# Float32 products with values, moved into one row behind their transpositions and copies

## The chip, the cores and the metric

The kernel runs on one core of one Trainium2 chip. The metric is the device time of one execution in microseconds, and the figure compared is the median over several executions. Five engines work side by side, each through its own queue and in the order of that queue: TensorE (PE in the profile; its weight loads are shown apart as PEld), VectorE (DVE), ScalarE (ACT), GpSimd (POOL) and SyncE (SP), which issues most of the transfers.

## The reference

A bidirectional encoder of two layers over 1024 tokens of width 1024, all in float32. What matters here is the mixing half of a layer: three groups of channels are computed side by side, normed, concatenated and projected.

```python
for l in range(DEPTH):
    h = _rmsnorm(x, g_pre_mix[l])
    zf, zq, zk, zv, zm = jnp.split(h @ w_in[l], splits, axis=-1)
    y_f = _fourier_mix(zf, w_fourier[l])
    q, k = _rope(zq), _rope(zk)              # 8 query heads, 2 key heads of 64
    y_a = _window_attn(q, k, v, sink[l])     # softmax(q k^T) v, window of 128 to each side, with a sink
    km, vm = split(_rmsnorm(mem, g_mem[l]) @ w_mem_kv[l])
    y_m = _memory_attn(zm, km, vm)           # softmax(q km^T) vm, 4 heads, 256 memory rows
    y = concat[_rmsnorm(y_f), _rmsnorm(y_a), _rmsnorm(y_m)] @ w_out[l]
    x = x + _rmsnorm(y, g_post_mix[l])
    gate, up = jnp.split(_rmsnorm(x) @ w_ffn_in[l], 2, axis=-1)
    x = x + _rmsnorm((silu(gate) * up) @ w_ffn_out[l])
```

## The kernel before

Tokens are cut into eight tiles of 128. Nearly every product is done as three products of float32 numbers split into a high and a low part (`split`, lines 174 to 177; class `Acc`, line 187). The products with values that this change touches are not: they multiply plain float32 operands, and the trace shows each of them as two records on PE, with 128 rows of operand and 64 columns of weight.

**Window attention.** The eight query heads form two groups of four, one for each key head. `att_units(g)` gives nine units per group; unit i forms the values of tile i-1 (`att_values`) and then the scores of tile i (`att_scores`). A tile sees nk blocks of keys, three, or two at the ends, so 22 blocks a layer. For each block j, PE transposes the four heads' probabilities into a PSUM tile `pT` (line 825, two buffers). In the first head group (g = 0) they are split and multiplied at line 840. In the second (g = 1), ScalarE copies them into one of four buffers `pf` (line 830), and for s = 0 and 1 a float32 product (line 833) adds the block's values into `av`: s = 0 writes partitions 0 to 63, s = 1 partitions 64 to 127, each 256 columns. ScalarE then takes `av` out (line 842), and `out_prep` splits it for the projection and forms its sum of squares (`ssp`, line 988).

**Memory attention.** Heads and halves of the sequence give eight score units (`mem_scores`); `mem_turn` transposes the exponentials of one head in two blocks of memory rows, mt = 0 and 1 (`mpT`, line 922), and ScalarE copies each (line 924). `mem_values(pr, half, pfs)` takes a pair of heads: four float32 products (line 932) add into `mav`, for mt = 0 and 1 and for s = 0 and 1 (the head of the pair, written to partitions 0 to 63 or 64 to 127), 512 columns each. VectorE takes `mav` out (line 933). There are four such pairs a layer.

**What sets the order.** The stages are interleaved by hand. The memory units stand beside the queries' projection (`qp`). The second head group runs in a loop that also holds, for earlier tiles, the output projection (`out`, shown as `mo`, line 187), the norms, and the transpositions for the feed-forward part (`hb.tile`, shown as `hTp`, line 1106). Within what dependencies allow, a planner then orders each engine's queue by simulated costs, work that comes earlier in the program first; an instruction that isn't ready by its costs is overtaken by later ones that are. That is how products of one tile come to stand apart on PE with other work between them:

```python
weave(mix.mem_units(), q[1:8] + [mix.fm_load] + q[8:])
...
for i in range(NT + 4):
    if i < NT + SKEW:
        att[i]()
    if 2 <= i < NT + 2:
        hs[i - 2] = mix.out(i - 2, x1d[i - 2])
    if i >= 4:
        hb.tile(hs.pop(i - 4), i - 4)
```

The accumulators of both products (`av`, `mav`) share two PSUM buffers with other users of the tag "av" (`ssp`, `qT`).

Of the kernel before, what the change touches and what calls it, by code (L numbers as in the profile page):

```python
# [19 lines left out]
P = 128  # L20
# [49 lines left out]
def tile_encoder(ctx: ExitStack, tc: tile.TileContext, T, C, out):  # L70
# [12 lines left out]
    def nm(s):  # L83
        uid[0] += 1
        return f"{s}_{uid[0]}"
# [49 lines left out]
    class Ring:  # L135


        def __init__(self, *ks):
            self.ks, self.i = ks, 0
# [28 lines left out]
    def ps(shape, name="ps", tag="pd"):  # L168
        return psp[tag].tile([P] + list(shape), F32, tag=tag, name=nm(name))

    f32 = lambda ap: ap.bitcast(F32)
    mm = nc.tensor.matmul

    def split(hi, lo, src, lo_eng=None):

        nc.scalar.copy(hi, src)  # L176
        return (lo_eng or nc.vector).tensor_tensor(out=lo, in0=src, in1=f32(hi), op=ALU.subtract)  # L177
# [334 lines left out]
                dup_stacks([(self.km[ci][:, j, 0], self.km[ci][:, j, 1]) for j in range(2)], raw[:, ci])  # L512


    class Mix:
        def __init__(self, l, hT, mem):
            self.l, self.hT, self.mem = l, hT, mem
# [299 lines left out]
        def att_values(self, g, n, es_, dst):  # L817

            k0, k1 = max(0, n - 1), min(NT, n + 2)
            nk = k1 - k0  # L820
            av = ps([512], "av", "av")
            for j in range(nk):
                pT = ps([4, P], "pT", "pT")
                for h in range(4):
                    nc.tensor.transpose(pT[:, h, :], es_[h // 2][:, h % 2, j * P : j * P + P], ident)  # L825
                if g:

                    pf = self.pfs[self.pfi % 4]
                    self.pfi += 1
                    nc.scalar.copy(pf, pT.rearrange("p (k s) q -> p s k q", s=2))  # L830
                    for s in range(2):
                        rhs = pf[:, s].rearrange("p k q -> p (k q)")
                        mm(av[64 * s : 64 * s + 64, 0 : 2 * P], self.v32[:, k0 + j], rhs, start=j == 0, stop=j == nk - 1)  # L833
                    continue
                pp = phs(2, 512, dt=F32R)
                ph, pl = pp[:, 0], pp[:, 1]
                split(ph, pl, pT.rearrange("p h q -> p (h q)"))
                lhs = self.vst[(k0 + j) // 4][:, (k0 + j) % 4, g].rearrange("p a d -> p (a d)")
                for i, p_ in enumerate((ph, pl)):
                    mm(av, lhs, p_, start=j == 0 and i == 0, stop=j == nk - 1 and i == 1)  # L840
            if g:
                nc.scalar.copy(dst, av[:, 0 : 2 * P].rearrange("p (k q) -> p k q", k=2))
            else:
                self.fold(av, dst)
# [82 lines left out]

        def mem_values(self, pr, half, pfs):
            av = ps([512], "mav", "av")
            for mt in range(2):  # L930
                for s in range(2):
                    mm(av[64 * s : 64 * s + 64], self.mem.v[:, mt, 2 * pr + s], pfs[s][mt], start=mt == 0, stop=mt == 1)  # L932
            nc.vector.tensor_copy(self.ym[half][:, pr, :], av)

        def mem_units(self):
# [483 lines left out]
    for l in range(DEPTH):  # L1419
# [4 lines left out]
        q = mix.skewed(mix.q, mix.q_turn, NT)  # L1424
# [142 lines left out]
```

## Time and profile before

| | |
|---|---|
| runs (median; lowest to highest) | 2031.55 us; 2031.51 to 2036.65 us |
| profiled execution: time, span | 2032.38 us, 2030.4 us |
| granted TensorE clock, mean over the span | 0.994 |
| VectorE, ScalarE, GpSimd busy | 74%, 52%, 34% of the span |
| memory attention with the queries' projection | about 145 to 210 us (layer 0), 1140 to 1210 us (layer 1) |
| second head group with the output projection | about 286 to 380 us (layer 0), 1285 to 1380 us (layer 1) |

The time of an execution is the span from the first to the last instruction and about 2 us around it. Busy time on PE counts the whole passage of a product through the array, so products that follow each other closely overlap in it; how long a row of them really holds PE is read from the chain of waits, or from the start of the first to the start of the next work.

### The profile page before, as it was taken

What the parts mean: (1) busy time and instruction counts of PE and PEld (TensorE: products, weight loads), DVE (VectorE), ACT (ScalarE), POOL (GpSimd) and SP (SyncE); (2) the same over time, 40 slices, a digit from 0 to 9 for tenths busy, and PEclk for the clock granted to TensorE, in tenths of its full rate; (3) what the DMA queues carried; (4) which work ended last, traced back from release to release, by engine and by line L of the source; (5) the groups of instructions that cost most, each with busy time, mean ns of one, the idle gap of its engine ahead of it and who ended that gap; (6) DMA issues with size and microseconds to landing.
All of it is one profiled execution on the core that took longest, in us unless ns stands there. A gap on an engine that the chain in (4) does not pass through costs nothing.

```text
span 2030.4 us, 28325 instructions
## 1 busy us (share of the span) xinstructions
PE 1984.7 (98%) x9587; PEld 1631.2 (80%) x9587; DVE 1492.6 (74%) x2346; ACT 1049.7 (52%) x2204; POOL 684.9 (34%) x811
## 2 busy tenths in 40 slices
PE   8999999999999999999999999999999999999998
PEld 7877878778888888887888778877788888887886
DVE  5566767897877776778876668679786776778766
ACT  6476877643333333554555768686333333346441
POOL 4344445224334333002423644451433433410011
PEclk9999999999999999999999999999999999999999
DMA  6110333434333324879831113244333323269973
GB/s 213 62 58 22 109 104 115 146 109 130 104 109 100 103 88 139 297 266 324 286 142 54 54 58 115 85 144 135 106 118 114 116 82 114 96 209 354 314 265 125
DMA packets 181889, 288.56 MB, mean 142 GB/s; under 512 B 15560, under 2 KB 81648, under 8 KB 181744
## 3 DMA queue, kind: packets, MB, share of 16 engines
q1 hardware_dynamic: 173680, 267.88, 39.7%
q10 hardware_dynamic: 8064, 18.88, 2.4%
q8 instruction: 75, 1.23, 0.2%
q14 instruction: 70, 0.57, 0.1%
HBM read 220.11 MB, written 66.58 MB: 141 GB/s over the span
## 4 chain that ended last, share of the span: by engine, by line
PE 86%; DVE 5%; DMA 3%; ACT 2%; issue 2%; POOL 1%; SPq 0%; DVEq 0%; POOLq 0%; ACTq 0%
PE fo L1330 17%; PE qc L1181 11%; PE qx L1181 11%; PE qy L1181 11%; PE mo L187 8%; PE qz L1181 5%; PE kvp L187 4%; PE qp L187 3%; PE zT L187 2%; PE sc L788 2%; PE pT L825 2%; PE av L833 1%; PE qa L1181 1%; PE mav L932 1%; PE av L840 1%
## 5 line engine op out<-in xcount | busy, mean ns | idle before, releaser
L1330 PE MATMUL fo<-arena_r 128*128 128x512 f32 x1512 | 354.2, 391 | 6.0 <-ACT big L1355 3.8
L1330 PEld LDWEIGHTS fo<-arena_r 128*128 128x128 f32 x1512 | 283.6, 188 | 65.6 <-ACT big L1355 4.6
L176 ACT CAST arena_r<-arena_f 128x512 fp32r<-128x512 f32 (+2 forms) x344 | 185.9, 571 | 179.5 <-DMA arena_f<-actd 66.6
L1181 PE MATMUL qc<-arena_r,flex 128*128 128x512 f32 x912 | 220.2, 390 | 0.0
L177 DVE TENSOR_TENSOR arena_r<-arena_f,arena_r 128x512 fp32r<-128x512 f32 x262 | 182.0, 727 | 46.9 <-ACT arena_r L176 39.0
L1171 ACT CAST flex<-arena_f 128x512 fp32r<-128x512 f32 x148 | 91.9, 621 | 235.0 <-PE qy L1181 73.3
L1181 PEld LDWEIGHTS qc<-arena_r,flex 128*128 128x128 f32 x912 | 171.2, 188 | 37.0
L1181 PE MATMUL qy<-arena_r,flex 128*128 128x512 f32 x576 | 139.9, 390 | 2.3 <-ACT flex L1171 2.3
L1171 ACT CAST arena_r<-arena_f 128x512 fp32r<-128x512 f32 x92 | 57.1, 621 | 159.1 <-DVE arena_f L1168 63.6
L1172 DVE TENSOR_TENSOR flex<-arena_f,flex 128x512 fp32r<-128x512 f32 x148 | 110.9, 750 | 28.4 <-ACT flex L1171 28.2
L1181 PEld LDWEIGHTS qy<-arena_r,flex 128*128 128x128 f32 x576 | 107.9, 188 | 25.3 <-ACT flex L1171 2.7
L1215 POOL TENSOR_TENSOR arena_f<-arena_f 128x512 f32<-128x512 f32 x36 | 47.3, 1315 | 237.5 <-ACT arena_f L1186 237.5
L1181 PE MATMUL qx<-arena_r 128*128 128x512 f32 x360 | 119.5, 389 | 0.0
L1181 PE MATMUL qy<-arena_r 128*128 128x512 f32 x480 | 116.7, 390 | 0.0
L1172 DVE TENSOR_TENSOR arena_r<-arena_f,arena_r 128x512 fp32r<-128x512 f32 x92 | 68.2, 742 | 63.2 <-ACT arena_r L1171 62.8
L1181 PE MATMUL qz<-arena_r,flex 128*128 128x512 f32 x320 | 106.8, 395 | 0.0
L1181 PEld LDWEIGHTS qy<-arena_r 128*128 128x128 f32 x480 | 90.3, 188 | 18.9 <-ACT arena_r L1171 0.2
L1168 DVE TENSOR_TENSOR arena_f<-arena_f 128x512 f32<-128x512 f32 x90 | 98.1, 1098 | 5.5 <-DMA arena_f<-in_w_ffn_in 3.9
L1222 POOL TENSOR_TENSOR arena_f<-arena_f 128x512 f32<-128x512 f32 x36 | 60.0, 1667 | 120.2 <-DVE arena_f L1221 120.2
L187 PE MATMUL mo<-big,arena_r 128*128 128x512 f32 x384 | 100.2, 399 | 0.3 <-ACT arena_f L1031 0.2
L1181 PE MATMUL qx<-flex,flex 128*128 128x512 f32 x304 | 100.1, 390 | 0.0
L1242 POOL TENSOR_TENSOR arena_f<-arena_f,flex 128x512 f32<-128x512 f32 x32 | 51.8, 1619 | 139.5 <-ACT flex L1233 83.7
(315 smaller groups left out, 4659.8 us busy)
## 6 DMA issues: line engine op xcount, KB each, us to landing
arena_f<-in_w_ffn_out SPq DMA_DIRECT2D x264, 256.0 KB, 4.7
actd<-arena_f SPq DMA_DIRECT2D x154, 256.0 KB, 2.5
arena_f<-actd SPq DMA_DIRECT2D x154, 256.0 KB, 4.4
arena_f<-in_w_ffn_in SPq DMA_DIRECT2D x46, 512.0 KB, 3.7
big<-in_w_ffn_in SPq DMA_DIRECT2D x40, 512.0 KB, 4.5
arena_f<-in_w_in SPq DMA_DIRECT2D x40, 256.0 KB, 2.9
arena_f<-in_x SPq DMA_DIRECT2D x16, 512.0 KB, 4.3
arena_f<-in_w_out SPq DMA_DIRECT2D x32, 256.0 KB, 2.7
```

The costliest lines, as they stand in the source:

```text
L176: nc.scalar.copy(hi, src)
L177: return (lo_eng or nc.vector).tensor_tensor(out=lo, in0=src, in1=f32(hi), op=ALU.subtract)
L187: mm(self.dst, a, b, start=self.i == 0, stop=self.i == self.n - 1)
L788: mm(pt, lhs, self.kst[g][i][:, k0 * P : k1 * P], start=i == 0, stop=i == 1)
L1168: nc.vector.tensor_tensor(out=s, in0=x, in1=y, op=op)
L1171: self.cast = nc.scalar.copy(w[:, 0], s)
L1172: nc.vector.tensor_tensor(out=w[:, 1], in0=s, in1=f32(w[:, 0]), op=ALU.subtract)
L1181: mm(pt, a, b, start=start and n == 0, stop=n == 11, skip_group_check=not start)
L1215: G(out=self.u2, in0=self.u2, in1=self.p1, op=ALU.add)
L1222: G(out=self.p5, in0=self.p1, in1=self.p5, op=ALU.add)
L1242: (G if i % 2 else V).tensor_tensor(out=a[i], in0=c, in1=g[i], op=ALU.mult)
L1330: mm(pt, ab[:, 0, x, sl], ab[:, 1, y], start=new and first and j == 0, stop=last and j == 2, skip_group_check=not new)
```

## The change

In the second head group, `att_values` first transposes and copies all blocks of the tile, keeping the copies in a list, and then issues the tile's products (four or six) one after the other, last block first. In `mem_values` the four products of a pair are issued in the order mt = 1, 0 and, within it, s = 1, 0. The first product issued is the one whose copy is made last. A new helper, `together`, sets the flags that open and close the accumulation: the first two products open the two halves of the partitions, the last two close them. The number and kind of instructions stay as they were.

```diff
+    def together(products):
+
+        for i, p_ in enumerate(products):
+            p_(i < 2, i >= len(products) - 2)
...
             av = ps([512], "av", "av")
+            pfs = []
             for j in range(nk):
                 pT = ps([4, P], "pT", "pT")
...
                     pf = self.pfs[self.pfi % 4]
                     self.pfi += 1
                     nc.scalar.copy(pf, pT.rearrange("p (k s) q -> p s k q", s=2))
-                    for s in range(2):
-                        rhs = pf[:, s].rearrange("p k q -> p (k q)")
-                        mm(av[64 * s : 64 * s + 64, 0 : 2 * P], self.v32[:, k0 + j], rhs, start=j == 0, stop=j == nk - 1)
+                    pfs.append(pf)
                     continue
...
             if g:
+                together([
+                    lambda start, stop, j=j, s=s: mm(
+                        av[64 * s : 64 * s + 64, 0 : 2 * P], self.v32[:, k0 + j], pfs[j][:, s].rearrange("p k q -> p (k q)"),
+                        start=start, stop=stop,
+                    )
+                    for j in reversed(range(nk)) for s in range(2)
+                ])
                 nc.scalar.copy(dst, av[:, 0 : 2 * P].rearrange("p (k q) -> p k q", k=2))
...
             av = ps([512], "mav", "av")
-            for mt in range(2):
-                for s in range(2):
-                    mm(av[64 * s : 64 * s + 64], self.mem.v[:, mt, 2 * pr + s], pfs[s][mt], start=mt == 0, stop=mt == 1)
+            together([
+                lambda start, stop, mt=mt, s=s: mm(av[64 * s : 64 * s + 64], self.mem.v[:, mt, 2 * pr + s], pfs[s][mt], start=start, stop=stop)
+                for mt in (1, 0) for s in (1, 0)
+            ])
             nc.vector.tensor_copy(self.ym[half][:, pr, :], av)
```

## The prediction

> **What bounds the kernel now.** I read the page first: the span, the engines, the chain.
>
> ```profile
> span 2030.4 us, 28325 instructions
> PE 1984.7 (98%) x9587; PEld 1631.2 (80%) x9587; DVE 1492.6 (74%) x2346; ACT 1049.7 (52%) x2204; POOL 684.9 (34%) x811
> PE 86%; DVE 5%; DMA 3%; ACT 2%; issue 2%; POOL 1%; SPq 0%; DVEq 0%; POOLq 0%; ACTq 0%
> ```
>
> TensorE is busy nearly all the time and carries 86% of the chain that ends last. Next, two stretches that hold the moved products, in the view of busy time by stretch:
>
> ```profile
> 160.00:180.00 20.00, 20.00 (x106) 14.38 (x106) 10.25 (x17) 10.04 (x32) 9.25 (x20) 1.00 0.00 1
> 290.00:372.00 82.00, 81.71 (x490) 64.03 (x488) 53.91 (x118) 60.57 (x154) 42.64 (x72) 1.00 0.33 115
> ```
>
> Behind the stretch stand its length and the busy time of PE, PEld, DVE, ACT and POOL. PE hardly rests, while the others have 20 to 50% to spare. So time that PE no longer spends here should reach the end, and time that another engine waits here costs nothing. Third, the moved products themselves: the attention's in the view of its tile, the memory part's in the view by stretch, one row a layer:
>
> ```profile
> L833 PE MATMUL av<-flex,arena_f x176: 379/379/431, 293.8 to 1369.1; 128*64 128x256 f32 x176
> ```
> ```profile
> 155.00:215.00 60.00, 11.17 (x32) 2.39 (x32) 1.00 0.11 36
> 1150.00:1215.00 65.00, 12.23 (x32) 2.57 (x32) 1.00 0.14 45
> ```
>
> A product has two records, so these are 88 products of 256 columns in attention and 16 of 512 columns in each layer's memory part, which now keep PE busy 11.17 and 12.23 us.
>
> **Two prices, from the chain of waits in order of time.** First the memory part of layer 0 (start, length, what; x2 of `mav` is one product):
>
> ```profile
> 168.29 1.01 PE mav L932 x4
> 169.30 0.59 PE mpT L922 x4
> 169.89 1.00 PE mav L932 x2
> ...
> 183.72 1.86 PE mav L932 x6
> ...
> 186.94 0.44 PE mpT L922 x4
> ...
> 198.57 1.87 PE mav L932 x8
> ...
> 205.13 1.00 PE mav L932 x2
> ```
>
> One product alone takes 1.00 us, two take 1.01, three 1.86, four 1.87. So the two that write different halves of the partitions run side by side, and PE is held by slots: 0.86 us (1.87 less 1.01) for a pair, and as much for a lone product. The rest of a piece, 1.00 - 0.86 = 0.14 us, is paid once for each stay in this shape of product.
>
> The second price is what a stay costs the work behind it. The four transposition records right behind a stay (169.30) take 0.59 us, four in peace (186.94) take 0.44: 0.15 us more. In attention:
>
> ```profile
> 286.11 2.76 PE mo L187 x12
> ...
> 293.89 0.58 PE av L833 x4
> ...
> 308.14 1.45 PE av L833 x12
> ...
> 1307.63 0.58 PE av L833 x4
> 1308.21 0.91 PE mo L187 x3
> ...
> 1368.93 0.58 PE av L833 x4
> ```
>
> Here x4 is one pair, x12 three: a pair takes (1.45 - 0.58) / 2 = 0.435 us, so a stay costs 0.145 us beside its pairs, as above. The three `mo` products behind it take 0.91 us, where twelve in peace take 2.76 (0.23 each): 0.22 us more. A stay therefore costs 0.145 + 0.15 = 0.30 to 0.145 + 0.22 = 0.37 us beside its slots. I take 0.33, as both kinds of work stand behind the groups. Weight loads and semaphores lie inside these pieces and aren't priced apart.
>
> **The change part by part.** It adds and removes no instruction, transfer or load; ScalarE's copies (lines 830, 924) and the copies out (842, 933) stay, and the queues of SP and POOL have no part in the moved products. What changes is how many stays there are and how well the slots are filled.
>
> (a) *Attention, second head group.* The chain shows 33 pieces of line 833 (16 in layer 0, 17 in layer 1; first and last quoted), all made of whole pairs. So no slot is gained. There are 16 tiles, each needs one stay: 33 - 16 = 17 stays go, 17 x 0.33 = 5.6 us. Bounds: 5.1 at 0.30, 6.3 at 0.37; nothing, if other work still cuts every tile's row.
>
> (b) *Memory, slots.* A row of four takes two slots. The pieces of layer 0, put to the four pairs of heads, hold 1+2+1, 1+3, 4 and 1+3 products, which is 3+3+2+3 slots; those of layer 1 hold 1+3 three times and 1+2+1, which is four times 3. The busy time above bears this out: 11 slots and 8 stays against 12 and 9 differ by one of each, 0.86 and about 0.2, and the rows by 12.23 - 11.17 = 1.06 us. So 23 slots against 16. Two of the seven I don't count: the lone first products of the last pairs, at 205.13 and 1204.01, fill a seam before attention in which other engines set the pace, as the timeline shows (in brackets the idle time before it, and what ended it):
>
> ```profile
> 208.70 0.58 PE L988 MATMUL ssp<-const,arena_f 128*128 128x2 f32 x4 [0.80 <-DVE arena_r L438]
> ```
> ```profile
> 1204.01 1.07 PE L932 MATMUL mav<-arena_f 128*64 128x512 f32 x2
> ```
>
> Moved from there, their 1.00 us becomes idle time. Five slots: 5 x 0.86 = 4.3 us.
>
> (c) *Memory, stays.* 8 and 9 become 4 and 4. Without the two of the seams seven go: 7 x 0.33 = 2.3 us.
>
> (d) *Waiting at the head of a row.* The first product of a row now waits for the last copy, and behind it on PE's queue wait its row and what the planner puts next (`mo`, `hTp`, `ssp`, scores). Before, each group waited for its own copy. What ended PE's idle time before line 833, weight loads included (total us, times), and the copy:
>
> ```profile
>   ACT arena_f L316: 0.5, 2
>   ACT arena_f L801: 0.5, 2
>   ACT arena_r L176: 0.3, 1
>   ACT arena_f L362: 0.2, 1
> ```
> ```profile
> L830 ACT COPY flex<-pT x44: 563/587/607, 290.4 to 1364.1; 128x512 f32<-128x512 f32 x44
> ```
>
> That is 1.5 us by ScalarE over 33 groups, 0.045 each; 24 rows at that rate are 1.1 us, no more than now. The cover is other PE work such as the 2.76 us at 286.11. Without it a row waits for one copy, 0.59 us. I take no change, nearest to the 0.045.
>
> (e) *Behind a row.* In attention the copy out (842) starts up to two pairs, 0.87 us, later after ScalarE's last copy than before. Who needs it is `out_prep`, and its result feeds an `mo` two tiles on; eight tiles fill the 82 us stretch, so that is some 20 us away. The `pf` buffers are read later too, but a buffer comes up again only with the next tile's second copy, some 10 us on. Both cost nothing while a tile takes that long; without that cover it would be 0.87 us a tile.
>
> (f) *Rows that don't hold.* Work earlier in the program that becomes ready can still get in between. Of 24 rows I expect two or three to be cut: 0.8 us back.
>
> Sum: 5.6 + 4.3 + 2.3 - 0.8 = 11.4 us. The profiled execution took 2032.38 us (its span and 2 us around it), 0.83 above the median of the runs. 2032.4 - 11.4 = 2021.0 for it; from the median 2031.55 it is 2020.1. I say 2020.
>
> **A rule weighed: the clock.** The kernel shows stretches of 3.4 us at half clock behind ones in which PE rested about half the time (the third last column is the granted clock):
>
> ```profile
> 370.50:374.00 3.50, 1.67 (x15) 1.16 (x12) 3.06 (x6) 2.24 (x6) 2.99 (x4) 1.00 0.62 199
> 374.00:377.40 3.40, 3.40 (x14) 3.02 (x13) 3.40 (x6) 2.14 (x4) 0.52 (x2) 0.50 0.70 189
> 205.80:209.20 3.40, 2.60 (x18) 1.93 (x17) 3.33 (x8) 2.77 (x5) 1.34 (x3) 1.00 0.46 150
> ```
>
> At half speed a stretch costs half of 3.40, 1.7 us. In the seam at 207 PE is busy 2.60 of 3.40 us; with the lone product gone from there the idle time comes near 0.80 + 1.00 = 1.8 us, and the first row has 3.50 - 1.67 = 1.83. So one more half-clock stretch is possible, and elsewhere one less: the sum would be 9.7 or 13.1. The Trainium skill ("TensorE: Matmul & The Clock Gate", Part 1) puts the half rate behind an idle window of about 3.4 us; by that a gap of 1.8 us costs nothing and the sum stays 11.4. The rows above contradict it: the clock fell after 1.83 us of rest.
>
> **The rivals.**
>
> *The rows are cut (faster or no change).* The planner orders PE's queue, so products may stay apart. If all attention rows are cut as now, (a) and its share of (f), 0.5, go: 11.4 - 5.1 = 6.3 us, 2025.3. For it: the 33 pieces for 16 tiles. Against: 308.14 x12 and 198.57 x8 are whole rows, where all copies were there; the new order makes that the rule.
>
> *The gain is given back (no change).* PE gets ahead and others become late: ScalarE with 60.57 us in 82, DVE and POOL with 10.25 and 9.25 in 20. For it: the seams, where the chain leaves PE already. Against: 0.29 us of idle PE in 82 us. If half is lost: 2031.55 - 5.7 = 2025.9.
>
> *Rows wait for their copies (slower).* PE's queue is in order. ScalarE's too: a last copy can stand behind exponentials (line 801 ended some of the waits above) or behind the copy before it. At one copy of 0.59 us for each of 24 rows, 14.2 us are lost against 12.2 won (before (f)): 2033.6. At two, 28.3: 2047.6. It decides from 0.51 us a row, and 0.76 make it slower by 0.3%. Against it: 0.045 us a group now, and that the last copy had to be waited for before as well.
>
> **How the numbers follow.** A measurement of this kernel tells about 0.3%, 6.1 us, from no change; faster means below 2025.4. The sum as worked out 0.66; rows cut 0.11, half of it on the faster side; given back 0.11; rows that wait 0.12, of which 0.10 beyond 0.3%. Faster 0.72, same 0.18, slower 0.10. Low end: all seven slots and nine stays of the memory part at 0.37 (6.0 + 3.3), (a) at 6.3 and one half-clock stretch less, 1.7: 17.3, so 2014. High end: the second rival with another half-clock stretch and half of (a) cut, 2030; what lies above is mostly the third.
>
> **What would show it.** Right: line 833 in 16 pieces of 1.01 or 1.45 us, line 932 in eight of 1.87, as many PE instructions as before; the feed-forward part of layer 0 starts about 5 us earlier, that of layer 1 about 11. Wrong: over 20 pieces of line 833; ScalarE ending more than 5 us of PE's idle time before it; more stretches at 0.50; DVE and ACT rising in the chain between 150 and 380 us. It fails above all if the new order moves what the planner places behind it, which nothing in the trace before can show.

## The result and the profile after

The changed kernel takes 2018.07 us (median of 6 runs, 2013.64 to 2025.46), the kernel before 2032.17 (6 runs): a ratio of 0.993, 95% interval 0.9914 to 0.9946. On a second chip session it was 0.9939 (0.9916 to 0.9962). Predicted were 2020 us and a range of 2014 to 2030. The page of the profiled execution, the fastest of the six with 2013.64 us:

```profile
span 2011.7 us, 28335 instructions
PE 1968.4 (98%) x9587; PEld 1627.5 (81%) x9587; DVE 1492.5 (74%) x2346; ACT 1049.0 (52%) x2204; POOL 686.2 (34%) x811
PE 83%; DVE 6%; DMA 3%; issue 3%; ACT 2%; POOL 2%; SPq 0%; DVEq 0%; POOLq 0%; ACTq 0%
```

PE has the same 9587 instructions and 16 us less busy time; the other engines are as they were. In the chain of waits every tile's products of attention (line 847 now) are one piece of two or three pairs, and every pair of heads of the memory part (line 942) one piece of two slots:

```profile
168.04 1.87 PE mav L942 x8
...
288.27 1.01 PE av L847 x8
...
297.12 1.45 PE av L847 x12
```

There are 16 stays in attention where 33 were, 8 in the memory part where 17 were, and none of the 24 rows is broken up. The memory part's products by themselves, one row a layer:

```profile
155.00:215.00 60.00, 7.75 (x32) 1.94 (x32) 1.00 0.13 41
1150.00:1215.00 65.00, 7.75 (x32) 1.94 (x32) 1.00 0.18 55
```

They were 11.17 and 12.23 us. To see where the time went, I divide both traces into stages at the last product of each kind. The four stages that hold the rows (length, then busy PE), first before, then after; in each fence the memory stage and the attention (both head groups) of layer 0, then the same two of layer 1:

```profile
124.50:211.00 86.50, 83.61 (x435) 64.03 (x434) 56.07 (x100) 56.04 (x145) 42.39 (x69) 0.98 0.15 47
211.00:370.70 159.70, 158.02 (x898) 129.26 (x898) 112.34 (x291) 122.06 (x321) 76.54 (x129) 1.00 0.33 115
1122.00:1209.50 87.50, 84.83 (x449) 64.60 (x449) 58.64 (x108) 61.06 (x162) 44.22 (x75) 1.00 0.16 50
1209.50:1369.10 159.60, 158.52 (x896) 128.17 (x896) 115.01 (x293) 121.77 (x319) 79.89 (x131) 1.00 0.34 115
```
```profile
122.70:206.10 83.40, 80.24 (x434) 63.18 (x432) 56.25 (x97) 55.65 (x144) 42.35 (x68) 0.98 0.17 51
206.10:362.40 156.30, 155.50 (x904) 129.60 (x900) 114.81 (x297) 122.24 (x322) 78.03 (x131) 1.00 0.35 117
1111.60:1195.60 84.00, 80.07 (x449) 63.78 (x447) 58.19 (x107) 60.94 (x165) 45.63 (x74) 1.00 0.17 54
1195.60:1354.10 158.50, 156.12 (x900) 129.48 (x898) 112.49 (x292) 118.66 (x313) 79.06 (x129) 1.00 0.34 112
```

Length less busy is PE's idle time. Memory stages: busy down by 3.4 and 4.8 us, idle up by 0.3 and 1.3, length down by 3.1 and 3.5. Attention: busy down by 2.5 and 2.4, idle down by 0.9 in layer 0 and up by 1.3 in layer 1, length down by 3.4 and 1.1. A little work crosses the boundary between the two: the four `ssp` records of each layer that stood before the last memory product (0.58 and 0.61 us) now stand behind it, and two records of scores have come ahead of it. Together the four stages gave 11.1 us. The rest of the trace's 18.7 is elsewhere, which is what the experiments had to explain.

### The profile page after: what moved, and what is told of

The parts are those of the page before. It is cut to its first block, busy times and chain, and to the rows that moved or that the text cites. A ratio compares the mean times of both kernels' runs of the same rounds, so it can differ in the third digit from the quotient of the medians.

```text
span 2011.7 us, 28335 instructions
## 1 busy us (share of the span) xinstructions
PE 1968.4 (98%) x9587; PEld 1627.5 (81%) x9587; DVE 1492.5 (74%) x2346; ACT 1049.0 (52%) x2204; POOL 686.2 (34%) x811
## 4 chain that ended last, share of the span: by engine, by line
PE 83%; DVE 6%; DMA 3%; issue 3%; ACT 2%; POOL 2%; SPq 0%; DVEq 0%; POOLq 0%; ACTq 0%
PE fo L1342 16%; PE qx L1193 11%; PE qy L1193 11%; PE qc L1193 11%; PE mo L187 7%; PE qz L1193 6%; PE kvp L187 4%; PE qp L187 4%; PE zT L187 2%; PE sc L793 2%; PE pT L831 2%; DVE arena_r L177 1%; PE qa L1193 1%; PE av L844 1%; DMA arena_f<-in_w_in 1%
```

## The experiments

The theory is that of the prediction: PE is held by slots and by stays, and what is taken from them reaches the end. The rivals are that the planner's new order of everything behind the change made the gain, or that other work of the execution did. All stage lengths below end at the same products as above. "Att + in" is both head groups of attention together with the feed-forward input, because work moves over that boundary; "rest" is the start, up to the last `kvp` product of layer 0, and both feed-forward outputs, where the order of the work is that of the kernel before. The stage of layer 1 up to its last `kvp` product is 83.1 us in every trace, and 9.1 us stand behind the last product; with these two a row of the table adds up to the span.

| trace (us) | memory, layers 0 and 1 | att + in, layers 0 and 1 | rest |
|---|---|---|---|
| before | 86.5, 87.5 | 593.7, 597.6 | 572.9 |
| after | 83.4, 84.0 | 589.6, 596.1 | 566.4 |
| the same again | 83.3, 83.8 | 591.1, 596.0 | 572.4 |
| attention only | 85.1, 88.5 | 595.5, 597.1 | 573.2 |
| attention only, again | 86.6, 89.5 | 595.4, 597.1 | 574.1 |
| attention, six tiles | 86.4, 87.4 | 592.2, 599.1 | 573.6 |
| memory only | 82.1, 85.3 | 595.1, 596.5 | 574.6 |
| first copy first | 86.8, 88.2 | 595.2, 597.5 | 574.4 |
| last pair as before | 83.9, 86.4 | 595.2, 599.1 | 568.1 |
| halves one after the other | 82.1, 84.8 | 594.5, 598.7 | 568.9 |
| rows cut | 83.6, 82.9 | 597.6, 597.8 | 574.4 |
| tail | 83.2, 83.2 | 595.0, 599.0 | 576.0 |
| rows in six tiles | 81.8, 85.8 | 593.5, 597.6 | 576.5 |

### The same kernel again

No edit.

> The changed kernel once more, for a second trace of it. By the theory (PE is held by slots of 0.86 and 0.435 us and by 0.33 us for each stay in the 64-column shape) the moved rows are worth 12 us, and the profiled execution's 18.7 us had some 6 us beside them that another execution need not have: an earlier start (1.8 us before any moved product) and stretches at half clock that were absent. So I expect 2015 to 2023 us, 24 whole rows again, and the time to go with the number of stretches at half clock. The rival, that the other 6 us come from the new order of the queues, expects them again in this trace: span near 2012 and no half-clock stretch behind the second head group of layer 0.

2020.09 us, ratio 0.9939 (0.9916 to 0.9962); the traced span is 2018.8 us. The queues carry the same work in the same order as in the first trace (but for two neighbours on ScalarE), and the memory and attention stages repeat within 0.2 us. The rest is 572.4 us, as before the change, where the first trace had 566.4. So of the first trace's 18.7 us, 6.5 belong to stages that the change doesn't touch, and 6.0 of these did not come again; 11.6 us did (2030.4 to 2018.8), 6.9 of it in the memory stages and 4.2 in attention and feed-forward input. Behind layer 0's attention a half-clock stretch shows how little it takes:

```profile
362.40:365.80 3.40, 2.17 (x21) 1.84 (x17) 3.40 (x6) 2.22 (x6) 1.83 (x3) 1.00 0.44 171
365.80:369.20 3.40, 3.40 (x17) 2.83 (x17) 3.40 (x7) 3.20 (x7) 1.31 (x3) 1.00 0.92 263
```
```profile
364.90:368.30 3.40, 2.18 (x20) 1.81 (x17) 3.40 (x6) 2.19 (x6) 1.86 (x3) 1.00 0.45 175
368.30:371.70 3.40, 3.40 (x10) 2.72 (x10) 3.40 (x7) 1.98 (x4) 1.30 (x3) 0.50 0.86 248
```

The first fence is the first trace, the second this one: the same work, 2.17 and 2.18 us of it in 3.40, and behind it the full clock once and half the clock once. The expected total and the 24 whole rows came. That the time goes with such stretches held in part only: between 60 and 2000 us the second trace has three of them and the first two, which is 1.7 us of the 7.1 between the traces. Most of the rest is 2.7 us at the start and 2.4 in layer 0's feed-forward output, where PE's idle time is 5.0 us instead of 3.2. The rival that the other 6 us come from the order of the queues is out.

### One part alone

```diff
# attention only: mem_values as before
# memory only: att_values as before
```

> Only the attention's products in rows; the memory part as before. The theory expects 17 stays fewer, 5.6 us: about 2026.5 us, with 16 pieces of the attention's product and 17 of the memory's. The rival, that the gain is a reshuffle of everything behind the change and not the stays, has no reason for a half: it allows anything from 2014 to 2034.

> Only the memory part's products in rows; the attention as before. The theory expects five slots and seven stays fewer, 6.6 us, and nothing from the two seams: about 2025.5 us, with the memory's product holding PE 7.75 us a layer instead of 11.2 and 12.2. With the attention's part alone it should add up to the whole. The rival that a lone product costs no more than half a pair (products are what counts, not slots) expects the stays alone, 2.3 to 3 us: 2029.

Memory only: 2027.6 us, 0.9976 (0.9959 to 0.9992), 4.9 us. Its memory stages are 4.4 and 2.2 us shorter (the second with a half-clock stretch more), near the 6.6 expected; 1.7 us of layer 0's 4.4 is a half-clock stretch absent. Attention only: 2034.66 us, 1.0008 (0.9992 to 1.0023). That is no gain at all, though it has its 16 pieces, and it contradicts the theory's 5.6 us. The parts don't add up: nothing and 4.9, but 12.4 for the whole change in the same session. In the attention stage PE did save time, but less than expected; in layer 1, where no work crossed the stage's ends, it is busy 156.57 us instead of 158.52:

```profile
1211.90:1370.20 158.30, 156.57 (x896) 129.51 (x896) 113.67 (x291) 119.77 (x315) 80.63 (x128) 1.00 0.33 113
```

That is 1.95 us for nine stays, 0.22 each. PE's idle time shows where the attention part lost time in layer 0 (timeline of the attention-only kernel; the idle time before in brackets):

```profile
381.03 0.84 PE L1192 MATMUL qa<-arena_r,flex 128*128 128x512 f32 x2 [2.66 <-ACT flex L1182]
...
441.59 0.74 PE L1192 MATMUL qz<-arena_r 128*128 128x512 f32 x2 [1.89 <-DVE arena_r L1183]
```
```profile
378.10:381.50 3.40, 0.74 (x4) 0.43 (x3) 3.40 (x5) 3.06 (x6) 2.21 (x3) 1.00 1.11 326
381.50:384.90 3.40, 3.40 (x12) 2.76 (x11) 2.68 (x5) 0.00 (x0) 0.80 (x2) 0.50 0.22 71
439.50:442.90 3.40, 1.51 (x7) 1.07 (x7) 3.40 (x5) 0.00 (x0) 1.49 (x1) 1.00 0.30 109
442.90:446.30 3.40, 3.40 (x10) 2.63 (x9) 1.48 (x3) 1.05 (x2) 0.00 (x0) 0.51 0.91 299
```

At the seam to the feed-forward part of layer 0 PE waits 2.66 us for a cast of weights that stands on ScalarE's queue behind late norms, then 1.89 us for VectorE, and each gap is followed by a stretch at half clock, 1.7 us. In the changed kernel the first of these gaps is 0.53 us; near the second a gap of 1.76 us stands there too, but with no half-clock stretch behind it. The products that moved lie 80 us ahead of the second gap. PE's queue there reads `hTp` 8, `qc` 12, `qa` 2, `hTp` 4 in the attention-only kernel, and `qc` 12, `qa` 2, `qc` 12, `qa` 10, `hTp` 8 in the changed one.

### First copy first

```diff
-                    for j in reversed(range(nk)) for s in range(2)
+                    for j in range(nk) for s in range(2)
...
-                for mt in (1, 0) for s in (1, 0)
+                for mt in (0, 1) for s in (0, 1)
```

> All products stand behind the tile's transpositions and copies in the program, as in the change, but the first copy's products come first (blocks and mt ascending, s = 0 before 1), as before the change. In the built program the planner then again sets the products apart, in 33 pieces in attention and 17 in the memory part. The theory expects no gain: 2030 to 2034 us. The rival that it is the place in the program, with fewer waits in each unit, that brought the gain expects 2018 to 2024.

2034.07 us, 1.0005 (0.9991 to 1.0018). In the trace all five engines run the same sequence of instructions as in the kernel before. So the place in the program is worth nothing by itself: the planner undoes it. What makes the rows is that the product whose copy is last comes first.

### Halves one after the other

```diff
+                for s in range(2):
+                    for j in reversed(range(nk)):
+                        mm(av[64 * s : 64 * s + 64, 0 : 2 * P], ...)      # and s = 1, 1, 0, 0 in mem_values
```

> The rows of the change in both places, but with the halves of the partitions one after the other: in attention all products of s = 0, then all of s = 1, in the memory part s = 1, 1, 0, 0. Neighbours then write the same half and can't run side by side, but where the halves change. By slots a memory row takes three slots instead of two (2.7 us instead of 1.87), an attention row of six takes five (2.3 us instead of 1.45), of four three (1.45 instead of 1.01). That is 8 x 0.86 + 12 x 0.87 + 4 x 0.435 = 19 us more work on PE than the change, so 2036 to 2040 us. The rival, that a stay's cost is all there is and neighbours' halves don't matter, expects the time of the change, 2018 to 2021.

2028.46 us, 0.9972 (0.996 to 0.9984): 19 us more than the change were expected; by the ratios there are 6.7, and PE's work in attention is up by 5. The chain of waits shows a memory row and an attention row of six:

```profile
166.94 1.87 PE mav L942 x8
...
296.16 1.93 PE av L848 x12
```

The memory row is as short as with alternating halves, and so is an attention row of four; only a row of three and three is longer, 1.93 us instead of 1.45. Attention's busy time is 158.08 and 158.59 us, 2.6 and 2.5 more than after the change, or 0.42 us for each of 12 long rows. Slots are right as a price (the halves do run side by side, or the rows would be 3.6 us long). That only neighbours can share a slot is wrong: PE starts a product of the other half past two of the same half, but not past three. The trace doesn't name the half that a record writes, so this takes it that the planner kept the program's order inside a row; the long row fits that order, as its second half starts 0.44 us behind the first, two records later.

### Rows cut on purpose

```diff
+                sp = ps([2], "spare", "av")
+                def spare():
+                    mm(sp, pfs[-1][:, 0, 0], ident[:, 0:2], start=True, stop=True)
...
+                    if j:
+                        spare()            # cut: between pairs; tail: as many behind the row
```

> The change, with 28 small extra products (two columns, full width of the array, into a PSUM tile that nothing reads) put into the attention's rows between pairs. In the built program the attention's products then stand in 36 pieces instead of 16. An extra product takes two records of some 0.11 us, 6 us in all, as in the next kernel. The theory expects 20 stays more than there, 20 x 0.33 = 6.6 us of work on PE in the two attention stages. The rival, that a stay costs only the 0.145 us inside its piece and the rest is hidden by the array's own pipeline, expects 2.9.

> The same 28 extra products, but behind the rows: 16 pieces of the attention's product as in the change. The comparison for the kernel with cut rows; by itself it should stand some 6 us (28 x 2 x 0.11) over the change.

Cut: 2030.08 us, 0.9983 (0.9971 to 0.9995). Tail: 2028.71, 0.9973 (0.9957 to 0.9989). The tail was expected some 6 us over the change: the ratios give 6.9, and PE's work in attention 4.9. The totals of cut and tail overlap; the stages tell them apart. Attention of layers 0 and 1, cut, then tail:

```profile
208.50:370.30 161.80, 161.42 (x930) 132.41 (x926) 116.06 (x296) 122.14 (x319) 78.84 (x130) 1.00 0.32 110
1207.70:1369.50 161.80, 160.46 (x926) 132.11 (x924) 112.25 (x295) 122.11 (x317) 80.75 (x132) 1.00 0.33 113
```
```profile
207.90:366.30 158.40, 158.04 (x928) 132.39 (x926) 115.23 (x295) 121.45 (x319) 79.37 (x129) 1.00 0.33 112
1208.80:1368.10 159.30, 158.52 (x926) 132.25 (x924) 113.23 (x292) 119.91 (x313) 79.26 (x129) 1.00 0.33 111
```

With the same instructions PE is busy 3.4 and 1.9 us longer for 20 stays more: 5.3 / 20 = 0.27 us a stay. In layer 0 one row was cut into five products and one, which is one slot of 0.435 us more; without it a stay costs 0.25. The rival's 0.145 is too little, my 0.33 too much. The change itself gives 4.9 us for 17 stays, 0.29, and the attention-only kernel 0.22 in layer 1.

### The last pair as before

```diff
+            if (pr, half) == (1, 1):
+                # the four products mt = 0, 1 and s = 0, 1 as before
```

> The change, but with the products of the last pair of heads (second half of the sequence) in their order of before, so that a lone product can stand ahead in the seam before attention: eleven pieces of the memory's product instead of eight. The prediction counted nothing for the two lone products in the seams. So the memory stage up to the last memory product should take as long as in the change within 0.5 us a layer, its PE work up by 1.2 us and its idle time down by as much. The rival, that the row helps in the seam too, expects it longer by 1.2 us in layer 0 and 1.5 in layer 1.

2029.84 us, 0.9987 (0.9973 to 1.0001). The memory stages are 83.9 and 86.4 us against 83.4 and 84.0, 1.7 us of the second being a half-clock stretch. Work on PE is up by 0.9 us in layer 0 and idle time down by 0.4; in layer 1 idle time didn't fall. So the lone product was worth little in the seam of layer 0, and some 0.7 us in that of layer 1: between theory and rival, not settled. What the run showed instead is larger than the question: two rows of 24 less (one a layer), and the kernel loses some ten of its twelve to fourteen microseconds. Its "att + in" in layer 0 is 595.2 us, as in the attention-only kernel, and its PE queue has that kernel's order at the seam. In layer 1 it is 599.1 us, 3.1 more than in the second trace of the change, and that seam has the same order of PE's queue in both; this part is not explained.

### Is it the seam?

```diff
-            if g:                      # rows of products
+            if g and n < 6:            # in short: tiles 6 and 7 add their products as before
```

> Attention alone again, with the memory part as before, but the last two tiles of each layer keep their products as before. In the built program the attention's products stand in 22 pieces (33 before, 16 in the attention-only kernel), and at the seam to layer 0's feed-forward part PE's queue reads qc 12, qa 2, qc 12, qa 10, hTp 8 as in the whole change, not hTp 8, qc 12, qa 2, hTp 4 as in the attention-only kernel. If the rows are worth 0.29 us a stay and the attention-only kernel lost its gain at that seam (idle gaps of 2.66 and 1.89 us and two stretches at half clock), this kernel with fewer rows is the faster of the two: 11 x 0.29 = 3.2 us under the kernel before, 2028 to 2031 us, with the attention and the feed-forward input of layer 0 together 2 to 4 us shorter than in the attention-only kernel. The rival, that attention rows alone give nothing because the time is set elsewhere, expects both at the time before.

> The attention-only kernel once more, for the comparison on the same chip and a second trace of it. If its seam is a matter of the queues' order, the gaps before qa and qz in layer 0 come again with some 2.7 and 1.9 us, and the time is that of the kernel before within 0.2%. If they were an accident of one execution (a late transfer), they are gone and the kernel is 3 to 5 us faster than before.

> The whole change but for the last two attention tiles of each layer, which keep their products as before: 21 pieces in attention, 8 in the memory part. By stays this is 5 x 0.29 = 1.5 us over the change, about 2021 us. But at the seam of layer 0 its queue is a third one (qc 12, qa 2, qc 12, qa 12, hTp 8), the one that the memory-only kernel has there. If that order costs the 4 us that the memory-only kernel's attention and feed-forward input took over the change's, it comes out at 2023 to 2027.

The edit above is that of the first and the third kernel; in the first the memory part is as before. The attention-only kernel, run again, came to 2034.7 us, 1.001 (0.9997 to 1.0022), with the same gaps as in its first trace and the same half-clock stretch behind:

```profile
384.43 0.77 PE L1192 MATMUL qa<-arena_r,flex 128*128 128x512 f32 x2 [2.62 <-ACT flex L1182]
...
445.00 0.74 PE L1192 MATMUL qz<-arena_r 128*128 128x512 f32 x2 [1.89 <-DVE arena_r L1183]
```
```profile
381.60:385.00 3.40, 0.78 (x3) 0.44 (x3) 3.40 (x5) 2.97 (x6) 2.23 (x3) 1.00 1.17 324
385.00:388.40 3.40, 3.40 (x11) 2.83 (x10) 2.68 (x5) 0.05 (x1) 0.71 (x2) 0.50 0.20 75
```

So these gaps belong to the queues' order and are no accident. With attention alone and rows in six tiles, layer 0's attention and feed-forward input take 592.2 us, 3.3 less than the 595.5 with rows in all eight, as expected from the other order at the seam. The total doesn't follow: 2035.0 us, 1.0016 (1.0004 to 1.0028), where 2028 to 2031 were expected. In the trace 3.0 us of this are layer 1's feed-forward input, 441.0 us (438.0 before), though PE's queue at that seam reads as it did before the change; the rest is open. The place in layer 0 is shown, then, and the price of that one order, 3 to 5 us; that the order at this seam explains the whole of the missing gain is not. The third kernel, the whole change but for two tiles a layer, takes 2026.93 us, 0.997 (0.9955 to 0.9985). That is the time expected of its order, and 5 us more than its five stays are worth. But its trace doesn't put them at that seam: layer 0's attention and feed-forward input take 593.5 us, 2.4 more than in the second trace of the change, and 4.1 us more stand in the rest, where the order didn't change.

## Why the prediction was right or wrong

*The two prices.* The slot of 0.86 us held: the memory rows take 1.87 us (two of the eight 1.89 and 1.94). A stay costs 0.22 to 0.29 us by three readings and not 0.33, under my lower bound of 0.30. The time that other work loses behind a stay was read from single pieces of the chain (0.15 and 0.22 us), and on average it is less.

*(a)* All 17 stays went. Busy time fell by 4.9 us where 5.6 were worked out; the price was too high. In the attention-only kernel the 17 stays went too, and the time didn't fall at all.

*(b), (c)* The sum, 6.6 us, is what the memory stages gave: 3.1 + 3.5, and 3.2 + 3.7 in the second trace. The seams took most of what the two lone products had given, as reckoned: busy time fell by 8.1 us (of it 1.2 are the `ssp` records that moved out) and idle time rose by 1.6.

*(d)* ScalarE ended 1.4 us of PE's idle time before line 847, against 1.5: heads of rows wait no longer than the groups did.

```profile
  ACT arena_f L316: 0.5, 2
  ACT arena_f L806: 0.5, 3
  ACT arena_r L176: 0.4, 1
```

The mechanism of the third rival, copies behind exponentials, did appear, but at another place: the next user of a transposition buffer waits until the late copies free it.

```profile
1341.94 0.66 PE L1118 MATMUL hTp<-const,arena_f 128*128 128x128 f32 x4 [1.02 <-ACT flex L836]
```

It is one of the gaps that made layer 1's attention give only 1.1 of its 2.4 us.

*(e)* ScalarE waits longer for the rows' last products, 5.5 us before its copies out instead of 2.4, and no idle time of PE is put down to these copies.

*(f)* No row was cut, so the 0.8 us were not lost there. An idle time of about that size is the wait just shown, which no term of the sum had. So the sum is near the measured time partly by luck: the stays were priced too high, and two small errors, the rows that weren't cut and this wait, cancel.

*The sum.* 11.4 us were predicted against one profiled execution. The second trace of the change is 11.6 below it, the timed ratios give 12.4 and 14.2, the first trace 18.7 with 6.5 us in stages that the change doesn't touch. Of the signs, the pieces and their lengths came as written; attention ends, and the feed-forward part starts, 8.3 us earlier in layer 0 and 15.0 in layer 1 in the first trace, 5.8 and 8.7 in the second, where 5 and 11 were written.

*What I left to the end* ("if the new order moves what the planner places behind it") is the larger effect. The queues of all engines differ in places from the first moved row up to the start of layer 1's feed-forward input (162 to 1387 us of the trace before). In the whole change the feed-forward inputs take about as long as before (433.3 and 434.9 us against 434.0 in layer 0, 437.6 and 437.5 against 438.0 in layer 1). Of the kernels with part of the rows, memory only fell short of the theory by some 2 us, the others by 5 to 10. My terms were about right for this kernel, but the chance of 0.66 for the sum as worked out was kind: of the five kernels with only part of these rows, none came within 5 us of the whole change's time, and two gained nothing.

*The clock.* Behind a rest of about a third of 3.40 us the clock fell in one execution of the same queues and not in the other. The Trainium skill ("TensorE: Matmul & The Clock Gate", Part 1) asks for an idle window of about 3.4 us; the stretches above with 0.74 and 1.51 us of work in 3.40 fell too, so the trace again disagrees. The page also calls the window free-running. The traces agree: in the trace before, stretches at half clock begin at 141.90, 374.00, 1438.96 and 1841.73 us, which are 68, 312 and 118 times 3.413 us apart, and in each other trace too they begin whole multiples of that apart. Counted in these windows, over the 13 traces between 60 and 2000 us and starting from the full clock, half clock followed each of 31 windows with less than 1.47 us of busy PE, some of those with 1.48 to 2.20, and none with more. The two outcomes are not settled by that: the window that holds the gap has 2.19 us of busy PE in both executions (361.92 to 365.33 us in the first, 364.87 to 368.28 in the second). It lies at the upper edge of what still fell, and what decided there is open.

## What to carry to other kernels

Products that use half of the array's columns cost by slots and by stays: issue them in one row, each with a partner on the other half, and put the one whose operand is ready last in front, so that nothing can come between. Where a planner orders the queues, price the moved work from pieces of the chain, but take the total as uncertain: here kernels with part of the change fell short of that price by 2 to 10 us. Check the seams behind it, stage by stage, before you believe or reject the change. Compare stages that the change can't touch first; here they alone differed by up to 10 us between traces.

## What the runs showed of the hardware

- PE runs products on the two halves of its columns side by side even when they aren't neighbours, if the rows stand in the program's order: with the order 1, 1, 0, 0 the row of four still takes 1.87 us; with three of one half ahead a row of six takes 1.93 us instead of 1.45.
- The clock changes on a grid of 3.413 us that is fixed within an execution. Windows of it with less than 1.47 us of busy PE were all followed by half clock (31 in 13 traces), windows with more than 2.20 us by none; the same work with 2.19 us of busy PE was followed by the full clock in one execution and half of it in another, 1.7 us of difference.
